# New cost figures for the planner of a hybrid encoder kernel: profiled durations in place of the old ones

## Chip, cores and metric

The kernel runs on one core of one Trainium2 chip. The metric is the device time of one execution in microseconds (us), lower is better. The engines are PE (matmul), DVE, ACT, POOL and SP, which issues the transfers.

## What is computed

Two sequences of 1024 tokens, 1024 wide, go through two layers with shared weights and a final RMSNorm. One layer, cut from the reference:

```python
hdn = rmsnorm(x, norm_g)
z = einsum('bsd,dp->bsp', hdn, w_in)      # 12 column blocks of 256
y_a = pool_mixer(a_v) * silu(a_g)         # multi-scale window means
y_b = dilated_attention(rope(b_q), rope(b_k), b_v) * silu(b_g)
y_c = s5_mixer(c_u) * silu(c_g)           # state-space scan, both directions, then a GLU
y_d = neighbourhood_attention(d_q, d_k, d_v, rpb) * silu(d_g)
return x + einsum('bsm,md->bsd', concatenate([y_a, y_b, y_c, y_d]), w_out)
```

Everything is 32-bit. The large products are made in three terms of a reduced type (fp32r): high times high, high times low, low times high.

## The kernel before

The work is four passes, numbered 0 to 3: layer 0 for both sequences, then layer 1 for both. In a pass the stages are recorded in this order (`STEPS`, L1659): neighbourhood attention ("na"), dilated attention ("dil"), the state-space scan ("ssm"), its GLU ("sout"), pooling, the next sequence's input, and the output projection in two halves. Passes 0 and 1 also hold a set-up of state-space tables for a layer (`ssm_setup`, L1181).

Nothing is issued while it is recorded. A `Recorder` notes every instruction with the tiles it reads and writes; `order()` (L304) then plays the program against five engines and a transfer queue and writes down in which order each engine gets its instructions; `emit` (L443) issues that order, every instruction from L461. Each engine executes its list strictly in that order, so a list is fixed before the chip sees it.

In that play an instruction holds its engine for `cost(op)` (L206), and a reader on another engine is ready `LAT` (L169) after that:

```python
op.end = now + op.cost            # L393
lat = LAT.get((e, o.eng), 130)    # L421
```

When an engine falls free it takes, of the instructions that are ready and whose tiles have room, the one of lowest priority number: its place in the recording, plus a large number (`LATE`, L475) for the long projections, which are so used as filler between the steps of the attention and scan chains. Filler is limited by tiles, by weights (three buffers of high parts, three of low) and by three PSUM banks; once issued it is gone for the stages behind it. `LAT` has, for instance, 142 ns from ACT to DVE, 127 from DVE to DVE and 640 from DVE to PE, and 1100 + 900 ns around a transfer.

The scan stage (`ssm_in`, L1444) works on four "quads" of groups in each pass. For a quad PE makes 16 products of `UM` and `B` into two PSUM banks (`pp`; the two banks of pool "s"). DVE reads them in four multiplications with `R` into `X` and a scratch tile, makes two sums and two scans over 512 columns, POOL multiplies `X` with `R` twice, DVE twice in place, and four DVE instructions write `H`. PE then multiplies `H` with `Cm` and `M` (the second half of `UM`) with `UM`. The set-up makes four groups: six DVE instructions of 512 columns for `W`, eight transposes of it on PE, six DVE instructions of 576 columns for `R`, eight small products of `R` on PE.

Names in profile and lists are those of the buffer's first user: `vz` is one of three PSUM banks for projections, `kt` one of two banks for scores and `pp`, `ss` and `rb` the two banks for transposes and for the scan's output, `no` the one for attention outputs; `xh`, `xl`, `whi`, `wlo` are halves of input and weight, and `wto`, `zq`, `zs`, `kt`, `th` also name the scratch tiles of 512 columns.

Of the kernel before, what the change touches and what calls it, by code (L numbers as in the profile page):

```python
# [176 lines left out]
class Recorder:  # L177
# [26 lines left out]
        self.threads.append(self.thread)  # L204

    def cost(self, op):  # L206
        out = op.writes[0]
        n = 1
        for _, c in out.dims[1:]:
            n *= c  # L210
        spaces = [v.tile.space for v in op.reads] + [out.tile.space]
        ps = "PSUM" in spaces
        if op.eng == "PE":
            if op.method == "transpose":
                return 107 * n / 128
            f32r = op.reads[0].dtype == F32R
            return n / 2.4 + 1 if f32r and n >= 256 else max(n, 128) / 0.6 + 1
        if op.eng == "DVE":
            m = op.method
            if m == "reciprocal":  # L220
                return 68 + 6.5 * n / 0.96
            if not ps and m in ("tensor_copy", "tensor_scalar", "tensor_scalar_mul", "memset"):
                return 66 + n * 0.525
            return 68 + n * 1.042 + (8 if m == "tensor_tensor_reduce" else 0) + (61 if isinstance(op.kw.get("scalar"), View) else 0)
        if op.eng == "ACT":
            return (52 if ps else 93) + n * 0.833 + (93 if "accum_out" in op.kw else 0) + (94 if len(op.reads) > 1 else 0)
        if op.eng == "POOL":
            if op.method == "memset":
                return 40 + n * 0.5
            spread = any(s == 0 and c > 1 for v in op.reads for s, c in v.dims[1:])  # L230
            return 148 + n * (1.67 if spread else 2.1)
        return 640

    def record(self, eng, method, args, kw):
# [243 lines left out]
SSMP, SB, GLU, POOLR, SPLIT, H0Z = (0, 1), "t", 0, 1, 'gpsimd', 1  # L478
# [1342 lines left out]
```

## Time and profile before

| | us |
|---|---|
| median of 3 runs (lowest, highest) | 2167.78 (2164.34, 2167.82) |
| the profiled execution | 2156.2 |
| its span, first to last instruction | 2154.4 |
| PE busy in the span | 1984.5 |
| DVE busy | 1572.2 |
| ACT busy | 1095.0 |
| POOL busy | 573.6 |

The busy time of PE is the union of matmuls whose recorded lengths overlap, so PE can be "busy" while it is fed at less than full rate. The table by stage further down sets each engine's busy time beside the length of the stage: the difference is idle time. A bracket in a timeline is idle time of that engine just before the row.

### The profile page before, as it was taken

The page shows a single profiled execution, that of the slowest core. Times are in us where ns is not written, and L with a number is a line of the kernel's source. Part 1 is how long each engine was busy: PE and PEld are TensorE (multiplying, and loading weights), DVE is VectorE, ACT ScalarE, POOL GpSimd, SP SyncE. Part 2 cuts the span into 40 slices and gives each one's busy share as a digit, 9 for nine tenths or more (in the row PEclk, how much of TensorE's full clock was granted, in tenths as well). Part 3 has the DMA queues.
Part 4 walks back from the last instruction along what each step waited for, and adds up shares of the span by engine and source line. Part 5 has one row for each costly group of instructions (what it writes and reads, how often), then busy time and mean ns, then how long its engine had stood idle before and what let it go on. Part 6 is the DMA issues. An engine that isn't in the chain of part 4 may idle for free.

```text
span 2154.4 us, 33356 instructions
## 1 busy us (share of the span) xinstructions
PE 1984.5 (92%) x10980; PEld 1656.8 (77%) x10980; DVE 1572.2 (73%) x3400; ACT 1095.0 (51%) x2486; POOL 573.6 (27%) x464
## 2 busy tenths in 40 slices
PE   7989999889999999889998999888899999998997
PEld 7757778667888888767787788767678878786777
DVE  7998688987246578788688667888734666888835
ACT  4438595134156688225125678823433766861315
POOL 3218231336200202124017142234543001202103
PEclk8999999999999999999999999999999999999999
DMA  4456535638855444646886543454588645346375
GB/s 160 147 167 188 169 95 169 191 106 269 270 168 160 134 145 118 202 134 217 265 250 187 175 151 105 129 180 155 197 283 278 214 144 173 106 139 201 115 243 178
DMA packets 321853, 381.12 MB, mean 177 GB/s; under 512 B 50832, under 2 KB 196752, under 8 KB 321680
## 3 DMA queue, kind: packets, MB, share of 16 engines
q1 hardware_dynamic: 321680, 378.99, 56.4%
q8 instruction: 87, 1.43, 0.3%
q14 instruction: 86, 0.70, 0.1%
HBM read 268.88 MB, written 112.10 MB: 177 GB/s over the span
## 4 chain that ended last, share of the span: by engine, by line
PE 44%; DVE 22%; DMA 14%; ACT 8%; issue 7%; POOL 3%; SPq 3%; DVEq 0%; POOLq 0%; ACTq 0%
PE vz L461 30%; DMA nv<-vd 4%; PE kt L461 4%; PE no L461 4%; DVE X L461 3%; DMA p<-x 3%; PE ss L461 3%; SPq L461 3%; PE rb L461 2%; DVE p L461 2%; DVE zq L461 1%; DVE gate L461 1%; DVE arena L461 1%; DVE H L461 1%; ACT p L461 1%
## 5 line engine op out<-in xcount | busy, mean ns | idle before, releaser
L461 PE MATMUL vz<-xh,whi 128*128 128x512 f32 x1324 | 531.7, 402 | 3.7 <-DVE zq L461 1.8
L461 PE MATMUL vz<-xl,whi 128*128 128x512 f32 x1324 | 531.5, 401 | 1.5 <-DVE xl L461 1.5
L461 PE MATMUL vz<-xh,wlo 128*128 128x512 f32 x1324 | 530.8, 401 | 0.8 <-POOL wlo L461 0.8
L461 POOL TENSOR_TENSOR wlo<-raw,whi 128x512 fp32r<-128x512 f32 x128 | 179.8, 1406 | 590.7 <-ACT whi L461 437.8
L461 ACT ACTIVATE whi<-raw 128x512 fp32r<-128x512 f32 x248 | 155.6, 627 | 340.5 <-DMA raw<-in_w_in 120.8
L461 PEld LDWEIGHTS vz<-xh,whi 128*128 128x128 f32 x1324 | 251.7, 190 | 49.9 <-issue 2.9
L461 PEld LDWEIGHTS vz<-xh,wlo 128*128 128x128 f32 x1324 | 251.8, 190 | 44.6 <-issue 2.1
L461 PEld LDWEIGHTS vz<-xl,whi 128*128 128x128 f32 x1324 | 252.2, 191 | 43.7 <-DVE xl L461 2.0
L461 PE MATMUL vz<-whi,xh 128*128 128x256 f32 x464 | 135.2, 292 | 15.1 <-ACT xh L461 8.6
L461 ACT ACTIVATE p<-p,st 128x256 f32<-128x256 f32 x256 | 128.3, 503 | 30.6 <-DVE st L461 29.3
L461 DVE TENSOR_TENSOR p<-vz,p 128x512 f32<-128x512 f32 x86 | 58.4, 687 | 112.8 <-DMA p<-x 96.8
L461 PE MATMUL vz<-whi,xl 128*128 128x256 f32 x464 | 134.2, 289 | 0.1
L461 PE MATMUL vz<-wlo,xh 128*128 128x256 f32 x464 | 133.8, 289 | 0.1
L461 PE MATMUL vz<-yh,whi 128*128 128x512 f32 x300 | 121.5, 405 | 9.6 <-DVE p L461 5.2
L461 PE MATMUL vz<-yl,whi 128*128 128x512 f32 x300 | 120.0, 400 | 0.0
L461 PE MATMUL vz<-yh,wlo 128*128 128x512 f32 x300 | 119.5, 400 | 0.0
L461 PEld LDWEIGHTS vz<-whi,xh 128*128 128x128 f32 x464 | 91.3, 197 | 16.9 <-ACT xh L461 8.6
L461 ACT ACTIVATE p<-p,nmx 128x384 f32<-128x384 f32 x128 | 78.2, 612 | 43.1 <-DVE nmx L461 42.1
L461 DVE TENSOR_TENSOR D<-ss,D 128x128 fp32r<-128x128 f32 (+2 forms) x195 | 85.5, 461 | 9.8 <-ACT D L461 8.2
L461 PEld LDWEIGHTS vz<-whi,xl 128*128 128x128 f32 x464 | 91.3, 197 | 1.0 <-issue 0.4
L461 PEld LDWEIGHTS vz<-wlo,xh 128*128 128x128 f32 x464 | 91.2, 197 | 0.8 <-issue 0.4
L461 PE MATMUL no<-D,bv 128*128 128x256 f32 x512 | 88.7, 293 | 3.1 <-DVE D L461 1.5
(489 smaller groups left out, 4616.1 us busy)
## 6 DMA issues: line engine op xcount, KB each, us to landing
raw<-in_w_in SPq DMA_DIRECT2D x192, 256.0 KB
low<-wlo SPq DMA_DIRECT2D x128, 256.0 KB
wlo<-low SPq DMA_DIRECT2D x120, 256.0 KB
x<-p SPq DMA_DIRECT2D x112, 256.0 KB
p<-x SPq DMA_DIRECT2D x88, 256.0 KB
nbias<-in_na_bias SPq DMA_DIRECT2D x48, 384.0 KB
nv<-vd SPq DMA_DIRECT2D x256, 64.0 KB
raw<-in_w_out SPq DMA_DIRECT2D x128, 128.0 KB
```

What stands on the lines that cost most here:

```text
L461: getattr(engines[op.eng], op.method)(*[real(a) for a in op.args], **{k: real(v) for k, v in op.kw.items()})
```

## The change

`cost` gets other figures, and nothing else is touched: not `LAT`, not the priorities, not the instructions. DVE gets 145 ns and 1.055 ns a column (68 and 1.042 before), 150 ns more where two operands of 256 columns or more lie in SBUF, 350 + 2.1 a column for a scan (priced like any other instruction before). ACT gets 180 or 205 ns of fixed cost (52 or 93 before). A 512-column matmul gets 226 ns (214 before), POOL 190 + 2.4 a column (148 + 2.1).

```diff
-        out = op.writes[0]
+
+        out, m = op.writes[0], op.method
...
         if op.eng == "PE":
-            if op.method == "transpose":
-                return 107 * n / 128
+            if m == "transpose":
+                return 108 * n / 128
             f32r = op.reads[0].dtype == F32R
-            return n / 2.4 + 1 if f32r and n >= 256 else max(n, 128) / 0.6 + 1
+            half = 0.7 if out.dims[0][1] == 64 else 1
+            return n / 2.4 + 13 if f32r and n >= 256 else half * (max(n, 128) / 0.6 + 9)
         if op.eng == "DVE":
-            m = op.method
+
+            wide = sum(v.tile.space == "SB" and v.dims[1:] != [[1, 1]] for v in op.reads) > 1
+            port = 150 if wide and n >= 256 else 0
             if m == "reciprocal":
-                return 68 + 6.5 * n / 0.96
+                return 145 + 6.1 * n
+            if m == "tensor_tensor_scan":
+                return 350 + 2.1 * n
             if not ps and m in ("tensor_copy", "tensor_scalar", "tensor_scalar_mul", "memset"):
-                return 66 + n * 0.525
-            return 68 + n * 1.042 + (8 if m == "tensor_tensor_reduce" else 0) + (61 if isinstance(op.kw.get("scalar"), View) else 0)
+                return 145 + n * 0.53
+            return 145 + n * 1.055 + port + (85 if m == "tensor_tensor_reduce" else 0) + (60 if isinstance(op.kw.get("scalar"), View) else 0)
         if op.eng == "ACT":
-            return (52 if ps else 93) + n * 0.833 + (93 if "accum_out" in op.kw else 0) + (94 if len(op.reads) > 1 else 0)
+            return (180 if ps else 205) + n * 0.833 + (187 if "accum_out" in op.kw else 0) + (88 if len(op.reads) > 1 else 0)
         if op.eng == "POOL":
-            if op.method == "memset":
-                return 40 + n * 0.5
+            if m == "memset":
+                return 90 + n * 0.84
             spread = any(s == 0 and c > 1 for v in op.reads for s, c in v.dims[1:])
-            return 148 + n * (1.67 if spread else 2.1)
+            return 190 + n * (1.8 if spread else 2.4)
```

The lists of all five engines change from their first rows on. Three places show how.

PE in the scan stage of pass 1, before: from the fourth quad's products to the row that reads the third quad's `H`.

```order
L461 MATMUL kt_1467<-UM_8725,B_8731 64x128 x8
L461 MATMUL vz_623<-UM_8725,B_8731 64x128 x8
L461 MATMUL vz_545<-xl_11_612,whi_644 128x512
L461 MATMUL vz_545<-xh_3_588,wlo_526 128x512
L461 MATMUL vz_545<-xh_4_663,whi_520 128x512
L461 MATMUL vz_545<-xl_12_679,whi_520 128x512
L461 MATMUL vz_545<-xh_4_663,wlo_792 128x512
L461 MATMUL vz_545<-xh_5_673,whi_520 128x512
L461 MATMUL rb_931<-H_8715,Cm_8710 128x128
```

Six projection matmuls stand here between the products and the first `H` row, and 65 between the third quad's first products and the fourth quad's `H`.

The same engine and stage after: the last row with the second quad's `H`, the fourth quad's products, the third quad's `H`.

```order
L467 MATMUL ss_693<-H_8685,Cm_8666 128x128 x2
L467 MATMUL vz_607<-UM_8807,B_8816 64x128 x8
L467 MATMUL kt_2298<-UM_8807,B_8816 64x128 x8
L467 MATMUL ss_693<-UM_8807 128x128
L467 MATMUL rb_940<-H_8805,Cm_8802 128x128 x2
```

The projection matmuls have gone from here to earlier places: the fourth quad's products are followed at once by the third quad's `H`, and 15 projection matmuls are left between the third quad's first products and the fourth quad's `H`.

DVE in that stage, before: from the fourth quad's second scan (the lists print a scan as SCALAR_TENSOR_TENSOR) to its `H`.

```order
L461 SCALAR_TENSOR_TENSOR X_8814<-zq_1100,X_8814 128x512
L461 TENSOR_TENSOR pu_8625<-vz_545,ss_4860 128x512
L461 SCALAR_TENSOR_TENSOR cs_8844<-cs_8844,cy_8811 128x1024
L461 TENSOR_TENSOR X_8814<-X_8814,R_1766_8737 128x512 x2
L461 TENSOR_TENSOR H_8807<-X_8814,zs_2230 64x4x127
L461 TENSOR_TENSOR H_8807<-X_8814,wto_1303 64x4x127
```

One instruction of pooling (`pu`) and one of the GLU stage (`cs`) stand here inside the chain.

DVE after: the fourth quad from its first sum, past both scans, to its `H`.

```order
L467 TENSOR_TENSOR X_8847<-X_8847,zs_2087 128x512
L467 SCALAR_TENSOR_TENSOR cs_8867<-cs_8867,cy_8849 128x1024
L467 SCALAR_TENSOR_TENSOR X_8847<-zq_1024,X_8847 128x512
L467 SCALAR_TENSOR_TENSOR cy_8849<-cs_8867,cy_8849 128x1024
L467 TENSOR_TENSOR wto_2167<-vz_607,R_1766_8824 128x512
L467 TENSOR_TENSOR X_8847<-X_8847,wto_2167 128x512
L467 SCALAR_TENSOR_TENSOR X_8847<-zq_1024,X_8847 128x512
L467 TENSOR_TENSOR X_8847<-X_8847,R_1766_8824 128x512
L467 SCALAR_TENSOR_TENSOR gate_7997<-zq_1024,zq_1367 128x512
L467 TENSOR_TENSOR X_8847<-X_8847,R_1766_8824 128x512
L467 TENSOR_TENSOR H_8875<-X_8847,zs_2087 64x4x127
L467 TENSOR_TENSOR H_8875<-X_8847,wto_2167 64x4x127
```

The `cy` instruction of the GLU stage, which stood behind the fourth quad's `H`, and a `gate` instruction now stand inside the chain; the third and fourth quads' steps are also interleaved more closely.

PE at the end of the first set-up, before: from a group's transposes of `W` to its products of `R`.

```order
L461 MATMUL rb_931<-c_ident_524,W_1778 128x128 x4
L461 MATMUL vz_543<-xh_6_722,wlo_792 128x512
L461 MATMUL vz_543<-xh_7_738,whi_520 128x512
L461 MATMUL vz_543<-xl_15_759,whi_520 128x512
L461 MATMUL vz_543<-xh_7_738,wlo_792 128x512
L461 MATMUL kt_1467<-R_1748,arena_630 32x128
L461 MATMUL kt_1467<-R_1810,arena_630 32x128
```

Projection matmuls stand here between a group's transposes and its products.

PE there after: the end of one group and the start of the next, its transposes and its first products.

```order
L467 MATMUL kt_2298<-R_2058,arena_614 32x128
L467 MATMUL kt_2298<-R_2404,arena_614 32x128
L467 MATMUL rb_940<-c_ident_524,W_2441 128x128 x8
L467 MATMUL kt_2298<-R_2422,arena_614 32x128
L467 MATMUL kt_2298<-R_2447,arena_614 32x128
```

The projections have moved ahead of this: the last three groups follow one another with none between.

## Rows read from the trace of the kernel before

**Rows 1.** Page, head and part 1: span, then busy time by engine.

```profile
span 2154.4 us, 33356 instructions
PE 1984.5 (92%) x10980; PEld 1656.8 (77%) x10980; DVE 1572.2 (73%) x3400; ACT 1095.0 (51%) x2486; POOL 573.6 (27%) x464
```

**Rows 2.** Page, part 4: the chain that ended last, by engine.

```profile
PE 44%; DVE 22%; DMA 14%; ACT 8%; issue 7%; POOL 3%; SPq 3%; DVEq 0%; POOLq 0%; ACTq 0%
```

**Rows 3.** Windows: start:end, length, busy PE, PEld, DVE, ACT, POOL, clock, DMA, GB/s.

```profile
45.00:160.00 115.00, 101.55 (x529) 80.32 (x528) 104.80 (x325) 48.73 (x108) 22.02 (x17) 0.94 0.53 155
160.00:365.00 205.00, 189.30 (x1166) 159.42 (x1165) 162.97 (x400) 155.44 (x406) 82.86 (x66) 1.00 0.49 148
365.00:440.00 75.00, 60.74 (x349) 50.22 (x349) 70.78 (x85) 11.39 (x21) 28.25 (x27) 0.94 0.59 188
...
610.00:880.00 270.00, 260.08 (x1515) 221.59 (x1514) 186.51 (x473) 193.33 (x491) 26.70 (x23) 0.99 0.47 138
880.00:950.00 70.00, 57.30 (x344) 48.19 (x343) 60.60 (x84) 11.53 (x19) 18.86 (x18) 0.93 0.60 196
...
1150.00:1405.00 255.00, 238.32 (x1388) 203.22 (x1389) 189.56 (x456) 186.40 (x480) 93.67 (x75) 0.98 0.47 146
1405.00:1490.00 85.00, 71.68 (x420) 57.99 (x417) 78.39 (x100) 13.99 (x24) 32.75 (x29) 0.96 0.55 169
...
1700.00:1925.00 225.00, 216.52 (x1285) 185.88 (x1283) 161.71 (x415) 171.49 (x442) 26.54 (x21) 0.99 0.47 140
1925.00:2000.00 75.00, 63.18 (x393) 52.19 (x392) 64.62 (x90) 11.84 (x21) 19.05 (x20) 0.93 0.61 191
```

**Rows 4.** Groups on PE, all forms apart: busy us, mean ns, idle before.

```profile
L461 PE MATMUL kt<-K,Qn 128*128 128x256 f32 x68 | 20.5, 315 | 8.2 <-ACT K L461 7.3 <-DVE st L461 0.5 <-ACT Qn L461 0.4
L461 PE MATMUL vz<-K,Qn 128*128 128x256 f32 x60 | 17.7, 310 | 3.4 <-ACT K L461 3.0 <-DVE st L461 0.3
```

**Rows 5.** Timeline of PE in pass 1: start, length, what, idle before.

```profile
895.19 1.09 PE L461 MATMUL vz<-UM,B 128*64 128x128 f32 x16
896.11 1.04 PE L461 MATMUL kt<-UM,B 128*64 128x128 f32 x16
...
913.00 0.39 PE L461 MATMUL vz<-xh,wlo 128*128 128x512 f32 x1
913.22 0.39 PE L461 MATMUL vz<-xh,whi 128*128 128x512 f32 x1
918.79 0.77 PE L461 MATMUL ss<-H,Cm 128*128 128x128 f32 x2 [5.18 <-issue]
...
922.26 0.61 PE L461 MATMUL ss<-H,Cm 128*128 128x128 f32 x4
922.70 0.39 PE L461 MATMUL ss<-UM 128*128 128x128 f32 x2
```

**Rows 6.** Timeline of DVE, same stage: start, length, what.

```profile
903.20 1.21 DVE L461 TENSOR_TENSOR bacc<-bacc,bacc 128x1024 f32<-128x1024 f32 x1
904.33 0.68 DVE L461 TENSOR_TENSOR X<-X,wto 128x512 f32<-128x512 f32 x1
...
933.36 0.68 DVE L461 TENSOR_TENSOR zs<-vz,R 128x512 f32<-128x512 f32 x1
933.96 0.68 DVE L461 TENSOR_TENSOR X<-vz,R 128x512 f32<-128x512 f32 x1
...
935.75 1.21 DVE L461 TENSOR_TENSOR_SCAN X<-zq,X 128x512 f32<-128x512 f32 x1
936.88 0.66 DVE L461 TENSOR_TENSOR X<-X,wto 128x512 f32<-128x512 f32 x1
```

**Rows 7.** All uses of tile X on DVE: duration min/median/max in ns.

```profile
L461 DVE TENSOR_TENSOR X<-X,R x32: 615/1512/1783, 374.1 to 1994.7; 128x512 f32<-128x512 f32 x32
```

**Rows 8.** Groups on DVE from 45 to 160 us: busy us, mean ns.

```profile
L461 DVE TENSOR_TENSOR W<-W,R 128x512 f32<-128x512 f32 x8 | 5.5, 682 | 0.1
L461 DVE TENSOR_TENSOR R<-R,W 128x576 f32<-128x576 f32 x8 | 6.5, 806 | 0.0
```

## The prediction

> **What bounds the kernel now.** I read the page's head and its chain first, then the busy time of each engine stage by stage, then single rows where a stage was idle.
>
> PE is busy 1984.5 of 2154.4 us and DVE 1572.2 [rows 1]; the chain that ended last lies 44% on PE, 22% on DVE and 14% on transfers [rows 2]. So PE sets the time overall, and what an order of the same instructions can win or lose is the time in which PE waits, 170 us. The table by stage says where that is [rows 3]. In the four stretches of scan, GLU and pooling (365 to 440, 880 to 950, 1405 to 1490 and 1925 to 2000 us) PE is idle 14.3, 12.7, 13.3 and 11.8 us, together 52.1; there DVE is busy 94, 87, 92 and 86% of the time: DVE is the bound, and PE keeps busy only as far as filler is left. In the four stretches of the attentions (160 to 365, 610 to 880, 1150 to 1405 and 1700 to 1925) PE is idle 15.7, 9.9, 16.7 and 8.5 us, together 50.8 of 955, with DVE at 69 to 79%. In the stretch of the first set-up (45 to 160) it is idle 13.5 us, DVE 91% busy. The other 54 us lie at the two ends and around the output projections.
>
> **What the new figures mean.** The profile shows a DVE instruction over 512 columns as 0.68 us long, but the next one starts 0.60 us after it: 933.36 and 933.96 [rows 6]. The old table has 68 + 512 x 1.042 = 602 ns for it, the spacing; the new one 685 ns with one operand in PSUM, 835 with two in SBUF, the recorded length and more. For a scan the old table has 602 ns, and the spacing is 1.13 us (935.75 to 936.88); the new one has 1425. For a 512-column matmul the spacing is 0.22 to 0.23 us (913.00 and 913.22) [rows 5]; here the new 226 ns is nearer than the old 214. The planner will thus rightly leave more room behind matmuls and scans, and wrongly believe DVE some quarter slower than it is. Filler goes wherever PE waits for a chain, so a plan with slower DVE spends more filler per step in the attentions, which come first, and has less for the scan, which comes last. The order shows that this is what happens.
>
> The Trainium skill speaks against this use of recorded lengths: Perfetto Trace Analysis, section Optimizing Scalar/DVE Operations, says that the recorded latency carries about twice the engine's overhead, because the write-acknowledging half overlaps the next instruction. The two DVE rows named above agree (0.68 long, 0.60 apart).
>
> **The sum, part by part.** Numbers of instructions are counted in the two orders, durations come from the rows.
>
> *Scan stage.* I take the piece between the third quad's first products on PE and the fourth quad's first `H` row, since DVE's work in it can begin only when those products end, and the `H` row can run only when that work has ended. Before, PE has 65 to 88 projection matmuls in this piece (15 to 20 us at 0.227) and DVE 35 to 40 instructions. After, PE has 15 in passes 1 to 3 and none in pass 0, and DVE has 41. What DVE needs: 33 instructions of 508 or 512 columns x 0.60 = 19.8; 3 of about 1024 columns x 1.13 (903.20 to 904.33) = 3.4; 5 scans x 1.13 = 5.7; together 28.9 us [rows 6]. What PE has: 15 x 0.227 = 3.4; 24 products of `UM` and `B` x 0.115 (895.19 to 896.11 for eight) = 2.8; 24 products with `H` or `M` x 0.22 (922.26 to 922.70 for two) = 5.3; 11.5 us, or 8.1 in pass 0 [rows 5]. PE must wait at least 17.4 us in each of three passes and 20.8 in pass 0: 73 us. On top come slower instructions. `X<-X,R`, two per quad, has a shortest length of 615 ns and a median of 1512 [rows 7]: it runs beside POOL's multiplications of the same tiles. Six of them in the piece x 0.83 us above the usual 0.68 = 5.0 a pass, 20 in all. So 93 us of waiting. The first two quads, which now have 18 to 27 us of PE work behind their products in place of 11 to 14, I take as covered. Against today's 52.1 us: **+41**. Lower end: no slowing, 73 - 52 = +21. Upper end: all six at the longest, 1783 ns, which is 6.6 a pass, and the first two quads keep a quarter of today's 52: 73 + 26 + 13 - 52 = +60.
>
> *Attention stages.* What left the scan stage covers waits here. The clearest one is the first scores of dilated attention, which wait 7.3 + 3.0 us for `K` from ACT [rows 4]: a quarter of them had under 12.8 us of PE work between the last projection of `K` and themselves, now only a tenth has under 24.5. I take all 10.3 us as saved. Of the remaining 40.5 us of idle time here I take a third, 13.5, since the work between a score and its transposes grows (median 7.4 to 8.4 us) but that between the transposes and the products that use them shrinks (5.0 to 4.2): **-24**. Ends: 10 us saved, or 40 (four fifths of all idle time there).
>
> *First set-up.* After, its last three groups stand on PE with no projection between. A group costs DVE 6 x 0.60 for `W` and 6 x 0.73 for `R` (682 and 806 ns long, 0.08 less as spacing [rows 8]), 8.0 us; its 16 small PE instructions, priced like those of the scan stage at 0.11, take 1.8. That leaves 6.2 a group, 19 for three, plus 2.5 for copies between: 21.5 against the 13.5 of today, **+8**. Ends: +3, if only 16.5 remain, and +18, if most of today's waits stay beside it.
>
> *The rest*: 0. SP issues the same transfers in another order. The PE work between a score that releases a load of `nv` and its use has a lower quartile of 16.5 us in place of 22, that ahead of a new projection weight 13.8 in place of 15.1; ACT's and POOL's figures move too, but neither engine is busy over 76% in any of the stretches read [rows 3]. I cover these by the 54 us of idle time outside the three kinds of stretch, which filler may shorten as well, and put 6 us either way.
>
> Sum: 41 - 24 + 8 = +25 us on the profiled 2156.2, hence 2181. That execution is 11.6 us under the median of the runs shown, 2167.78, which I take as the base: **2193 us**. By the lengths of the rows in place of their spacings the scan piece would be 41 x 0.08 = 3.3 us a pass longer, 2206.
>
> **Rivals.**
>
> *Faster: more room pays more than it costs.* The waits of the attentions fall by four fifths (-40), the set-up stays even, and the scan stage only reaches its lower end (+21): -19, 2149 us. For it: 51 us of idle time lie in stages that get filler, and scans and matmuls are now priced nearer the truth. Against it: the 73 us of the scan stage follow from counts and spacings alone. It decides once the saving in the attentions exceeds what the scan stage adds.
>
> *Same: filler only moves waits.* A scan stage at its lower end (+21), the attentions at the forecast (-24), the set-up at +3: 2168.
>
> *Slower still: the scan stage starves what follows.* GLU and pooling read what these chains make and have no filler of their own; if the first two quads keep half their waits (+26) beyond the forecast: 2219. For it: the granted clock in these stretches is 0.93 to 0.96 against 0.98 to 1.00 in the attentions [rows 3], so idle time costs some speed after it. It counts within slower.
>
> **How the numbers follow.** The forecast and the case beyond it have 0.70 (0.55 and 0.15), the faster rival 0.19, the same 0.11. About 0.2%, 4.3 us, is what a measurement of this kernel can tell from no change. The lower ends together give 21 - 40 + 3 = -16, with the 6 us of the rest -22; the upper ones 60 - 10 + 18 + 6 = +74. A tenth of the chance on each side is cut off: -12 to +60, 2156 to 2228.
>
> **What would show it.** The scan stretches should show 80 to 110 us of idle PE in place of 52.1, nearly all ahead of the third and fourth quads' `H` rows, in two waits a pass of 6 to 12 us, with DVE busy throughout. The attention stretches should show under 35 us of idle time and almost none on the scores that wait for `K`; around the last set-up groups three waits of about 6 us. I am wrong if the waits ahead of the last `H` rows sum to under 60 us, or if the attentions lose more idle time than the scan stages gain.

## The result, and the profile after

The changed kernel takes 2246.94 us (median of 4 runs, 2242.42 to 2252.87) beside 2166.06 us for the kernel before on the same chip (4 runs, 2162.55 to 2167.82): a ratio of 1.0382, 95% interval 1.0351 to 1.0412. It is slower by 81 us, where 25 were forecast and the range ended at 2228.

The head of the page, after; it answers to [rows 1]:

```profile
span 2251.1 us, 33433 instructions
PE 1997.8 (89%) x10980; PEld 1679.9 (75%) x10980; DVE 1580.2 (70%) x3400; ACT 1110.7 (49%) x2486; POOL 590.6 (26%) x464
```

The instructions are the same, and PE is busy 13.3 us longer and idle 83.4 us longer (253.3 in place of 169.9); the two make up the 96.7 us by which this span is longer than that of [rows 1]. The medians differ by 81 only: of the two profiled executions the one before lies 9.9 us under its median and the one after 5.9 over. The chain that ended last can be followed back only to 586 us here, so that its shares sum to 74% and can't be set beside those of [rows 2].

For the ledger the spans are cut where the work changes, not at equal times: at the first product and at the last output product of each scan. First the kernel before (columns as in [rows 3]; pass 0 up to the scan, the attentions of passes 1 to 3, and by itself the first set-up):

```profile
0.00:358.00 358.00, 315.98 (x1829) 266.20 (x1830) 294.56 (x802) 218.98 (x534) 122.90 (x101) 0.96 0.51 155
...
579.00:872.00 293.00, 283.08 (x1686) 244.77 (x1684) 186.91 (x475) 200.91 (x506) 28.18 (x23) 0.99 0.49 146
...
1094.00:1404.00 310.00, 291.40 (x1747) 247.97 (x1745) 239.64 (x584) 202.13 (x509) 106.56 (x84) 0.98 0.53 161
...
1629.00:1925.00 296.00, 286.03 (x1708) 247.59 (x1706) 201.11 (x502) 203.69 (x512) 34.18 (x28) 0.99 0.55 170
...
78.00:146.00 68.00, 61.61 (x332) 46.50 (x329) 62.75 (x131) 29.45 (x64) 10.79 (x8) 0.96 0.48 129
...
sum 323.00, PE 270.91 PEld 222.72 DVE 287.92 ACT 54.19 POOL 99.73; mean PE 67.73 PEld 55.68 DVE 71.98 ACT 13.55 POOL 24.93
```

The last row is the sum of the four scan stretches (358 to 444, 872 to 948, 1404 to 1490 and 1925 to 2000 us): PE is idle 52.1 us in them, as in the stretches of [rows 3].

The same view of the changed kernel, with its four scan stretches:

```profile
0.00:380.00 380.00, 330.77 (x1894) 282.76 (x1896) 302.16 (x802) 223.28 (x531) 131.04 (x104) 0.92 0.50 153
380.00:474.00 94.00, 57.63 (x354) 48.28 (x355) 71.21 (x101) 14.76 (x31) 26.82 (x24) 0.80 0.38 122
...
608.00:912.00 304.00, 295.04 (x1734) 256.87 (x1733) 188.88 (x470) 200.62 (x495) 30.62 (x24) 0.99 0.49 151
912.00:1006.00 94.00, 62.51 (x364) 51.31 (x364) 69.24 (x100) 15.48 (x30) 20.70 (x20) 0.79 0.40 124
...
1145.00:1471.00 326.00, 307.93 (x1817) 263.31 (x1817) 257.68 (x601) 203.58 (x500) 116.73 (x88) 0.98 0.54 164
1471.00:1563.00 92.00, 60.38 (x363) 49.72 (x360) 73.31 (x102) 15.76 (x32) 28.05 (x24) 0.80 0.39 124
...
1702.00:2007.00 305.00, 296.36 (x1758) 257.93 (x1757) 203.78 (x498) 202.06 (x498) 33.90 (x27) 1.00 0.54 172
2007.00:2099.00 92.00, 60.30 (x361) 49.44 (x362) 68.56 (x100) 15.21 (x31) 19.75 (x20) 0.81 0.40 125
...
139.00:217.00 78.00, 53.97 (x344) 42.96 (x342) 65.94 (x129) 36.20 (x75) 19.37 (x15) 0.81 0.44 117
```

Idle PE is length less busy PE, in us:

| stage | before | after | difference |
|---|---|---|---|
| four scans | 52.1 | 131.2 | +79.1 |
| first set-up | 6.4 | 24.0 | +17.6 |
| the rest of pass 0 up to its scan | 35.6 | 25.2 | -10.4 |
| attentions of passes 1 to 3 | 38.5 | 35.7 | -2.8 |
| all else | 37.3 | 37.2 | -0.1 |

So nearly all of it is the scan, and the saving in the attentions, which should have paid for a good part, is almost absent. In the scan stretches DVE is busy 74 to 80% of the time, less than before [rows 3], and PE's granted clock is 0.79 to 0.81 in place of 0.93 to 0.96.

The idle time is not spread evenly over a scan. Sums of the four stretches, first up to the third quad's first products (423.96, 955.61, 1512.51 and 2048.71 us), then from there on:

```profile
sum 170.79, PE 146.72 PEld 114.91 DVE 125.89 ACT 37.95 POOL 39.09; mean PE 36.68 PEld 28.73 DVE 31.47 ACT 9.49 POOL 9.77
...
sum 201.21, PE 94.11 PEld 83.84 DVE 156.41 ACT 23.27 POOL 56.23; mean PE 23.53 PEld 20.96 DVE 39.10 ACT 5.82 POOL 14.06
```

PE is idle 24.1 us in the first parts and 107.1 in the second, where it was 18.2 and 33.9 before, cut in the same way.

PE's timeline in the scan of pass 1, after: start, length, what, and in brackets the idle time before it.

```profile
955.61 1.09 PE L467 MATMUL kt<-UM,B 128*64 128x128 f32 x16
...
959.95 0.39 PE L467 MATMUL vz<-xh,wlo 128*128 128x512 f32 x1
...
967.67 1.35 PE L467 MATMUL ss<-H,Cm 128*128 128x128 f32 x4 [5.89 <-issue]
...
976.35 1.97 PE L467 MATMUL kt<-UM,B 128*64 128x128 f32 x16 [2.52 <-DVE zq L467]
980.46 0.77 PE L467 MATMUL ss<-UM 128*128 128x128 f32 x2 [2.14 <-DMA UM<-Md]
984.30 1.35 PE L467 MATMUL rb<-H,Cm 128*128 128x128 f32 x4 [3.07 <-issue]
...
1001.00 1.35 PE L467 MATMUL ss<-H,Cm 128*128 128x128 f32 x4 [11.51 <-issue]
...
1005.85 0.78 PE L467 MATMUL vz<-xh,whi 128*128 128x512 f32 x1
```

The last filler before the gap is the projection at 959.95, the next one starts at 1005.85. Between them PE has the products of the last quads and waits. The rows at 967.67, 984.30 and 1001.00 begin the output of the second, third and fourth quad. The chain of waits over the same stretch says for what (start, length, what):

```profile
967.67 5.15 PE ss L467 x22
...
972.89 0.61 ACT zq L467
...
973.51 2.00 DMA yd<-zq
...
975.60 0.70 DVE zq L467
...
977.15 2.20 POOL zq L467
...
979.37 1.74 DVE X L467
...
984.30 5.21 PE rb L467 x22
...
989.59 0.61 ACT wto L467
...
990.21 2.00 DMA yd<-wto
...
992.31 0.70 DVE wto L467
...
1001.00 5.19 PE ss L467 x22
```

The quads run one behind the other. PE's output products of a quad end, ACT copies them into a scratch tile (`ys`, here under the name `zq`, then `wto`), a transfer reads that tile (2.00 us), and only then may DVE write the same tile as `H0` of the next quad, whose `H` PE waits for. From 967.67 to 984.30 and on to 1001.00 the rounds take 16.6 and 16.7 us, 5.2 of them PE's own products.

The gates of GLU and pooling and the input of pooling have 288 projection matmuls in a pass. Where the two orders put them on PE, over the four passes:

| | ahead of the scan's first product | in the scan | behind it |
|---|---|---|---|
| before | 0 | 150 to 179 | 109 to 138 |
| after | 61 to 71 | 97 to 107 | 120 |

By this count the scan lost 43 to 75 projections a pass and 61 to 71 went ahead of it, so the filler did move early. But about as many as before, 120, or 27 us of PE a pass at 0.227, still lay behind the scan while PE stood idle in it, and these were not drawn in. Something in the plan held them back. A gate's projection leaves its PSUM bank into a scratch tile (`zg`), one of the six from which the scan's chain takes `H0`, `r8b` and `ys`; then ACT needs a second scratch tile (`th`) to go on. Three gate halves of the GLU stage show it in pass 1, after. DVE empties the bank into the scratch tile in the first three rows, and ACT reads that tile in the last three (`ss` is the name of the tile of scales here):

```profile
895.60 0.69 DVE L467 SCALAR_TENSOR_TENSOR zq<-vz,ss 128x512 f32<-128x512 f32 x1 [0.19 <-PE vz L467]
...
905.68 0.69 DVE L467 SCALAR_TENSOR_TENSOR th<-vz,ss 128x512 f32<-128x512 f32 x1 [0.34 <-PE vz L467]
...
931.81 0.69 DVE L467 SCALAR_TENSOR_TENSOR zr<-vz,ss 128x512 f32<-128x512 f32 x1
...
995.15 0.63 ACT L467 ACTIVATE zq<-zq 128x512 f32<-128x512 f32 x1 [4.96 <-DVE X L467]
998.45 0.63 ACT L467 ACTIVATE zq<-th 128x512 f32<-128x512 f32 x1 [2.67 <-DVE gate L467]
1001.58 0.63 ACT L467 ACTIVATE wto<-zr 128x512 f32<-128x512 f32 x1 [2.51 <-DVE H L467]
```

They hold three of the six tiles for 99.6, 92.8 and 69.8 us and can't go on, while the scan uses the other three or the plan keeps them for it. In `order()`'s own play two of the three banks stay full behind them and the third is left empty, so that no other projection begins; in its play of the kernel before, no gate there waits over 7 us for its second tile.

### The profile page after: what moved, and what is told of

It reads as the page before. It is cut to its first block, busy times and chain, and to the rows that moved or that the text cites. A ratio compares the mean times of both kernels' runs of the same rounds, so it can differ in the third digit from the quotient of the medians.

```text
span 2251.1 us, 33433 instructions
## 1 busy us (share of the span) xinstructions
PE 1997.8 (89%) x10980; PEld 1679.9 (75%) x10980; DVE 1580.2 (70%) x3400; ACT 1110.7 (49%) x2486; POOL 590.6 (26%) x464
## 3 DMA queue, kind: packets, MB, share of 16 engines
q1 hardware_dynamic: 321680, 378.99, 53.4%
## 4 chain that ended last, share of the span: by engine, by line
PE 44%; DMA 13%; DVE 9%; issue 3%; SPq 2%; ACT 2%; POOL 1%; DVEq 0%; ACTq 0%; POOLq 0%
PE vz L467 30%; PE kt L467 4%; DMA nv<-vd 4%; PE no L467 4%; PE ss L467 3%; DMA p<-x 3%; PE rb L467 3%; SPq L467 2%; DVE X L467 1%; DVE gate L467 1%; DVE p L467 1%; DMA bf<-f 1%; DVE xl L467 1%; DVE bacc L467 1%; DMA p<-in_x 1%
## 5 line engine op out<-in xcount | busy, mean ns | idle before, releaser
L467 PE MATMUL vz<-whi,xh 128*128 128x256 f32 x432 | 125.4, 294 | 10.9 <-ACT xh L467 8.7
L467 PE MATMUL vz<-whi,xl 128*128 128x256 f32 x432 | 126.0, 292 | 0.7 <-DVE xl L467 0.6
L467 PE MATMUL vz<-wlo,xh 128*128 128x256 f32 x432 | 125.5, 292 | 0.0
L467 DVE TENSOR_TENSOR D<-rb,D 128x256 fp32r<-128x256 f32 (+2 forms) x220 | 94.2, 448 | 15.9 <-ACT D L467 12.5
L467 ACT ACTIVATE D<-rb 128x256 fp32r<-128x256 f32 (+2 forms) x220 | 83.5, 406 | 28.0 <-PE rb L467 24.8
L467 PE MATMUL ss<-H,Cm 128*128 128x128 f32 x128 | 34.9, 425 | 69.9 <-issue 57.8
L467 PEld LDWEIGHTS vz<-whi,xh 128*128 128x128 f32 x432 | 85.9, 200 | 12.5 <-ACT xh L467 8.7
L467 PE MATMUL rb<-c_ident,p 128*128 128x128 f32 x490 | 87.7, 277 | 3.3 <-ACT p L467 3.3
```

The lines of the kernel that those rows point to most:

```text
L467: getattr(engines[op.eng], op.method)(*[real(a) for a in op.args], **{k: real(v) for k, v in op.kw.items()})
```

## Experiments

Theory A: the filler that is left is held up by scratch tiles, as just told. Theory B: the prediction's, filler spent because DVE is believed slow. The kernels that mix the tables hold both bodies of `cost`, as `old_cost` and `new_cost`, and choose by engine or by stage; their diffs show that one line. "Idle" is PE idle in the four scan stretches, cut as in the ledger (52.1 before, 131.2 after).

| run | us | ratio to before (95% interval) | idle |
|---|---|---|---|
| new_gate_in_place | 2198.28 | 1.0154 (1.0107 to 1.0200) | 27.5 |
| old_gate_in_place | 2173.52 | 1.0034 (1.0015 to 1.0054) | 54.0 |
| new_act_only | 2292.64 | 1.0587 (1.0552 to 1.0621) | 129.7 |
| new_dve_only | 2182.07 | 1.0065 (1.0045 to 1.0084) | 58.0 |
| act_gate_in_place | 2168.86 | 0.9999 (0.9977 to 1.0022) | 53.4 |
| new_attn_only | 2229.14 | 1.0275 (1.0226 to 1.0324) | 106.6 |
| new_not_attn | 2139.10 | 0.9872 (0.9825 to 0.9918) | 15.9 |
| new_setup_scan | 2129.60 | 0.9825 (0.9787 to 0.9864) | 13.6 |
| new_ys_in_X | 2190.83 | 1.0114 (1.0084 to 1.0144) | 89.8 |
| act_dil_only | 2266.40 | 1.0469 (1.0440 to 1.0499) | 127.3 |
| new_scan_only | 2130.59 | 0.9835 (0.9804 to 0.9865) | 17.2 |
| setup_scan_less_scratch | 2129.73 | 0.9847 (0.9810 to 0.9884) | 14.8 |
| all_but_act_dil | 2183.12 | 1.0093 (1.0064 to 1.0122) | 32.0 |
| new_less_scratch | 2214.49 | 1.0236 (1.0211 to 1.0261) | 21.8 |
| spacing_table | 2193.84 | 1.0131 (1.0101 to 1.0161) | 43.9 |

**Is the filler spent or held up?** All new figures, and a gate that needs no scratch tile to empty its bank:

```diff
-            z, th = self.z("zg"), self.z("th")
+            z, th = g[:, sl], self.z("th")
```

> All new figures, and one tile less: a gate's projection is scaled out of its PSUM bank into the gate's own tile instead of into a scratch tile. Theory A (held up): in the changed kernel the projections of the gates and of pooling were not spent early; they stood still because a bank can only be emptied into one of the six scratch tiles, which the scan's chain held, so that all three banks stayed full. The bank now needs no scratch tile; the order has 82 to 117 projection matmuls (0 before) behind the third quad's products and 86 to 91 behind the fourth's. It expects PE idle in the four scan stretches of 60 us or less in place of 131, and 2165 to 2205 us in place of 2247. Theory B (the prediction's: filler spent early in the attentions, 73 us of wait owed to DVE's work alone): what was spent does not come back, the waits move, 2235 to 2255.

The control is the same edit on the old figures.

> Control: the old figures with the same one tile less. Both theories: the scratch tiles were not short in the old plan, so 2166 within 8 us. If this is faster by 15 us or more, the edit helps by itself and the other run says less about the figures.

50 of the 81 us come back (31 are left over before on the same chip); the control is 0.3% slower. Windows of the run with the new figures, the scan of pass 1 and what stands behind it up to the next pass:

```profile
899.00:988.00 89.00, 81.59 (x494) 67.47 (x490) 78.01 (x117) 23.91 (x46) 18.66 (x22) 0.96 0.57 177
988.00:1135.00 147.00, 123.63 (x533) 95.50 (x534) 108.97 (x272) 45.35 (x69) 36.98 (x21) 0.92 0.64 205
```

PE runs 494 matmuls in this scan in place of 364, idle 7.4 us in place of 31.5. In this order 57 to 65 projections a pass still stand ahead of the scan, but 223 to 231 within it and none behind. So theory A holds for the scan, with one correction: projections did go ahead, and it is not these that the scan lacked, but those that were held up. The price is in the second row: 23.4 us idle behind the scan, where 7 were lost before and after, because with no projection left nothing stands beside the GLU; the waits of PE over the whole run show it (us in total, times, longest):

```profile
PE vz L467 <- DMA gw<-in_glu_w: 26.4, 4, 8.1
```

**Which engine's figures?**

```diff
+        return self.new_cost(op) if op.eng in ('ACT',) else self.old_cost(op)
```

(with `'DVE'` in the second run, and with the gate in place besides in the third)

> New figures for ACT alone (180 or 205 ns fixed in place of 52 or 93), old ones for all others. Theory A (held up by the gate's chain DVE - ACT - DVE, which holds a scratch tile from its first to its last instruction): ACT's figures alone lengthen that hold; the order has only 7 to 19 projection matmuls behind the third and the fourth quad's products. It expects 2200 to 2245 us, with scan stretches of 80 us or more of idle PE. Theory B (prediction: DVE believed too slow is what moves filler): within 15 us of 2166.

> New figures for DVE alone, old ones for all others. Theory B (prediction): this is the cause, so most of the +81 us: 2215 to 2250. Theory A: in this order the third and fourth quads of passes 1 to 3 have 91 to 107 projection matmuls behind their products, only pass 0 has 0 and 18; it expects one starved scan stage of four, about 20 us, and up to 15 us at the set-up: 2180 to 2205.

> New figures for ACT alone, and the gate's projection scaled into the gate's own tile. Theory A (held up): with ACT alone the waits lay in pooling (its weights' high halves come late from ACT, since the three buffers stay full while the projections before them stand in full banks). Without the scratch tile the order has 46 to 67 projection matmuls behind the third and the fourth quad's products: from 2293 back to 2165 to 2200 us, and the 30 us that pooling's projections wait in each pass fall under 10. Theory C (ACT's figures hurt by another way, such as where its weight splits stand in its own list): 2240 us or more.

DVE's figures, on which the prediction argued, cost 15 us. In the run with them alone one scan stretch of four starves, as expected: 45 of the 58 us of idle time are in pass 0. ACT's figures alone cost 126, more than all together and more than theory A had allowed: PE is idle 276 us in all (2008.3 busy of 2284.2), 106 more than before, of which 78 lie in the scans. The gate edit brings that run back from 2292.64 to 2168.86, with idle time in the scans at 53.4, as before: for ACT's figures by themselves the scratch tile is all of it. PE's and POOL's figures were not tried alone.

**Which stage?**

```diff
+        return self.new_cost(op) if op.thread.name.startswith(("na_", "dil_")) else self.old_cost(op)
```

(the complement has `not` in front; the others name `("ssm_","setup")`, `"ssm_"`, and ACT in `"dil_"`)

> New figures for the instructions of neighbourhood and dilated attention only, old ones elsewhere. Theory B (the prediction's: attentions that are believed slow spend the filler): all of it comes from here, 2230 us or more, with the attentions' waits down by 20 us. Theory A: the order has no projection behind the third and 19 behind the fourth quad's products in passes 0, 1 and 3, but 68 and 79 in pass 2; the hold-up needs a gate that begins inside dilated attention and then finds its scratch tiles taken, which these figures bring about: 2195 to 2240.

> The complement: new figures everywhere but in the two attentions. Theory A and B: filler is kept for the scan (the order has 64 to 108 projection matmuls behind the third and the fourth quad's products in place of 24 to 55): faster than 2166, 2130 to 2160. Theory D (the scan's, set-up's and pooling's own new figures do harm): 2175 or more.

> New figures only in the set-up and in the scan stage: what the change would be if only the two stages in which DVE is the bound were repriced. The order has 65 to 109 projection matmuls behind the third and the fourth quad's products. Theory A: scan waits fall from 73 to under 45 us, set-up waits to under 10, nothing else moves: 2125 to 2155. Theory D: 2166 or more.

> New figures in the scan stage alone; the set-up keeps the old ones. The order has 64 to 107 projection matmuls behind the third and the fourth quad's products (before: 26 to 55). Scan waits 73 down to 25 to 45 us, set-up unchanged: 2130 to 2160. If the gain of the run with both (2129.6) came from the set-up: 2160 or more.

> New figures for one engine in one stage: ACT in dilated attention; old ones elsewhere. Theory A (the plan then sees PE idle in dilated attention, begins the next gates there, and they are the ones that find their scratch tiles taken): the order has 58 to 91 gate and pooling projections ahead of the scan's first products (none with the old figures) and 0 to 10 behind the third quad's: 2225 to 2290, as bad as all new figures together. If the scan's or pooling's own figures were needed for the loss: 2185 or less.

The stages fall on opposite sides. New figures in the attentions alone cost 61 us, and ACT's in dilated attention alone 99 us (the first of the two runs lies just where the expectations of A and B meet and decides little; the second shows that ACT's figures in one stage are enough for the loss). Everywhere but in the attentions they gain 29, in set-up and scan alone 38, in the scan alone 37. The orders say how: with ACT repriced in dilated attention 58 to 91 gate and pooling projections stand ahead of the scan and 100 behind it; with set-up and scan repriced none stands ahead, 219 to 233 within and 55 to 69 behind. The scan of pass 1 in the run with set-up and scan repriced (windows):

```profile
875.00:953.00 78.00, 77.54 (x475) 64.57 (x475) 70.87 (x103) 17.46 (x28) 18.58 (x22) 1.00 0.65 206
```

PE is idle for 0.5 us in it, DVE busy 91%. This version, the new table in the set-up and the scan only, beats both kernels, the one before by 1.8%; with the scan alone repriced the time is the same within the noise.

**Is that trigger needed?** All new figures except ACT's in dilated attention:

```diff
+        return self.new_cost(op) if not (op.eng == "ACT" and op.thread.name.startswith("dil_")) else self.old_cost(op)
```

> All new figures but one engine in one stage: ACT in dilated attention keeps the old ones. Theory A (that is the trigger, and needed): the order has 10 gate and pooling projections ahead of the scan's first products (61 to 71 in the changed kernel) and 25 to 60 behind the scan (120): the scan's waits fall from 156 to under 70 us; set-up stays where it is; 2165 to 2205. If the other figures hold the gates up as well: 2225 or more.

62 of the 81 us go with it (19 are left over before on the same chip), and idle time in the scans falls to 32.0.

**Why was the scan's wait larger than its work?** All new figures, with `ys` in a tile that is dead by then:

```diff
-            ys = self.z("ys")
+            ys = X[:, 0]
```

> All new figures; the copy of the scan's output (ys) goes into the first half of X, which is dead by then, and no longer into a scratch tile that the next quad's H0 must wait for until the transfer yd<-ys has read it. The filler is as in the changed kernel: no projection behind the third quad's products in pass 0, 15 in the others, none behind the fourth's; DVE's work is the same. Theory S (the scan's wait was undersized because each quad waits for the scratch tile of the one before, so that DVE's work starts late): 25 to 60 us less than the changed kernel, 2185 to 2222, with DVE busier in the scan stretches than the 66 to 71 us of 87 to 90 it has now. Theory W (the wait is DVE's own work plus half clock on PE after each wait): within 12 us of 2247.

57 us less, with the same fillers in the same stretches. Windows of its four scans, to be set beside those of the changed kernel:

```profile
382.00:463.00 81.00, 56.75 (x348) 47.58 (x347) 66.36 (x92) 14.94 (x31) 25.57 (x24) 0.81 0.46 141
900.00:980.00 80.00, 56.99 (x362) 46.36 (x362) 66.18 (x92) 15.73 (x31) 18.97 (x18) 0.89 0.48 143
1436.00:1515.00 79.00, 57.94 (x362) 47.68 (x361) 68.22 (x93) 16.44 (x34) 25.52 (x24) 0.85 0.47 144
1959.00:2039.00 80.00, 58.51 (x365) 47.96 (x364) 65.12 (x93) 15.89 (x31) 20.16 (x20) 0.86 0.47 146
```

12 to 14 us shorter each, idle 89.8 together in place of 131.2, DVE busy 81 to 86%. So 41 us of the idle time hung on that one tile, which ACT's copy and the transfer hold until the next quad may write it, and not on DVE's work. All of it lies from the third quad's first products on, where PE is idle 64.6 us in place of 107.1; ahead of them it is 25.2 in place of 24.1. The same edit on the kernel before was not tried.

**Do the parts add up?** Both edits on all new figures, and both on the fastest mixture:

> All new figures with both edits, gate in its own tile and ys in X: what the figures cost where scratch tiles are not short. The order has 0 to 4 of 288 projections left behind the scan, so nothing covers the GLU: its waits stay near the 69 us of the run with the gate alone. 2185 to 2205, about that run's 2198; under 2180 if the scratch tiles were all of it.

> New figures in set-up and scan, the gate in its own tile and ys in X: the best of the pieces together. If the scratch tiles still bound the scan with these figures: 2100 to 2125. If the figures alone had freed them already (55 to 69 of 288 projections are left behind the scan in either case): 2125 to 2140, the same as without the two edits.

They do not. Idle time in the scans is lowest of the runs with all new figures, 21.8, and the time is worse than with either edit alone. Sum of the windows of the four stretches behind the scans (462 to 592, 983 to 1130, 1542 to 1690 and 2064 to 2208 us):

```profile
sum 569.00, PE 461.83 PEld 350.99 DVE 360.63 ACT 190.60 POOL 168.77; mean PE 115.46 PEld 87.75 DVE 90.16 ACT 47.65 POOL 42.19
```

PE is idle 107 us there. Nearly all filler went into the scan or ahead of it (0 to 4 projections a pass are left behind it), and the stages behind starved instead. With the mixture the edits change nothing: with its figures the scratch tiles were not what bound the scan.

**Are lengths in place of spacings the fault?** DVE by the old table, but a scan at its spacing, ACT nearly by the old table, PE and POOL as in the change (the lines of DVE's other instructions, not shown here, go back to the old figures):

```diff
-                return 350 + 2.1 * n
+                return 58 + 2.1 * n
...
-            return (180 if ps else 205) + n * 0.833 + (187 if "accum_out" in op.kw else 0) + (88 if len(op.reads) > 1 else 0)
+            return (52 if ps else 108) + n * 0.833 + (93 if "accum_out" in op.kw else 0) + (88 if len(op.reads) > 1 else 0)
```

> A table by the spacing from one start to the next: DVE and ACT as in the old table, but a scan at 1.13 us and ACT reading SBUF at 108 ns plus 0.833 a column; PE and POOL as in the change. If the loss came from recorded lengths taken for spacings, as the prediction's premise has it: 2150 to 2172. If any shift of the figures loses the old table's luck: 2185 or more.

A miss for the first expectation: 30 us slower than before, though idle time in the scans is 43.9. The time lies in the range of the other one, that any shift of the figures loses what the old order had; that not every shift does is shown by the runs that gain. PE is busy 18 us longer and idle 18 us longer (2002.5 of 2190.7), the latter spread over the other stretches. A table that is nearer to the spacings is not better by that. Why this one loses was not followed further; PE's and POOL's new figures are in it.

## Why the prediction was wrong in size and in cause

By spans 25 us were forecast and 96.7 measured. Of the 71.7 between them 38 are in the scan's term, 11 in that of the attentions, 10 in the set-up's and 13 in PE's busy time, which had no term.

**Direction and place were right**: slower, and by the scan. Ahead of the third and the fourth quads' `H` PE waits 79.6 us over the four passes, above the 60 under which the prediction called itself wrong; 11.5 a pass lie ahead of the fourth, and the rest is in several pieces ahead of the third. In time the slower rival, 2219, was nearer than the forecast. Of what it rests on, the first two quads keep waits, but its GLU does not starve (idle time behind the scan of pass 1 is 7.5 us before and 6.9 after).

**The cause was not.** The step "filler goes wherever PE waits for a chain, so a plan with slower DVE spends more filler per step in the attentions" failed twice. The figures that matter are ACT's, 126 us alone against 15 for DVE's; and of them those in dilated attention, 99 us. I had read that "ACT's and POOL's figures move too", and put it into the rest at 0 because neither engine is busy; but a planner's figures act by the order they make, not by how busy the engine is. And what was spent early is not what the scan lacked. 61 to 71 projections a pass did move ahead, yet 120 stood behind the scan, and making the gate independent of the scratch tiles brought idle time in the scans to 27.5 with 57 to 65 still ahead. I had counted the projections in the one piece and never asked where the others stood. The Trainium skill's Perfetto Trace Analysis, section Identifying Performance Opportunities, says that the same gap repeating on the engine that should be saturated can mean that there is too little SBUF or PSUM for the next tile. The trace agrees: the gap ahead of the last quad's products (11.51 us in pass 1) comes in every scan, and an edit of one tile takes 104 of 131 us away. The scratch tiles and banks can be counted in the program beforehand.

**Scan stage, +41, measured +79.** The forecast's 93 us of idle time are for the piece from the third quad's first products on; measured there are 107. The other 24 us lie ahead of that piece, in the part of the first two quads that the sum took "as covered", at nothing. The 93 are near the 107 by luck, since two terms inside were wrong and offset each other. The hand-over of the scratch tile was left out: without it 64.6 us are left in the piece. And DVE was to be "busy throughout", with `X<-X,R` at its slow length in every quad of the piece; DVE is busy 156.4 of 201.2 us there, 78%, and the median of `X<-X,R` fell from the 1512 ns of [rows 7] to 691. Its row among the uses of tile X on DVE, after:

```profile
L467 DVE TENSOR_TENSOR X<-X,R x32: 671/691/1745, 411.4 to 2091.0; 128x512 f32<-128x512 f32 x32
```

**Attentions, -24, measured -13.** -10.4 are in pass 0 (with its start), -2.8 in the three others together. Filler there covered little. Waits of PE, after (us in total, times, longest):

```profile
PE rb L467 <- DVE W L467: 13.1, 5, 4.8
...
PE kt L467 <- DVE R L467: 8.7, 8, 2.3
PE kt L467 <- ACT K L467: 7.6, 4, 3.2
```

The last row was to be gone. With 0.9 us of the `vz` group, 8.5 of the 10.3 us of [rows 4] are still there. More PE work between a projection and its score, as the order shows it, took 1.8 us off these waits and not 10.3.

**Set-up, +8, measured +17.6.** The first two rows are the waits named, `W` and `R`, 21.8 us, in thirteen pieces and not in three. The mechanism was right: 24.0 us of idle time where 21.5 were forecast. The term was mis-sized by what was taken off, the 13.5 of a stretch of 115 us that held other work too; in the set-up itself only 6.4 had been idle.

**The rest, 0**, measured -0.1 in idle time. One term was not in the sum at all: PE is busy 13.3 us longer with the same instructions. Its cause stays open. The mean granted clock fell from 0.975 to 0.945, but PE's busy time does not follow it from run to run: with the spacing table it is 18 us longer at 0.972, and with `ys` in X it is that of the kernel before, 1984.2, at 0.959.

**Lengths against spacings.** The rows still show it, 0.68 long and 0.60 apart [rows 6], as the Trainium skill's Perfetto Trace Analysis, section Optimizing Scalar/DVE Operations, has it. But the use I made of it does not follow: DVE's longer figures cost little, and the table by spacings was slower as well.

## What to carry to other kernels

When a planner's figures move, don't stop at "filler is used earlier": count it ahead of, in and behind the stage that starves. If some is left behind an idle engine, look for what it must own to begin (a bank, the scratch tile that empties the bank, and the tile after that) and who holds it. A wait is bounded by the engine's work only if the buffers of successive rounds are free; follow one tile through copy, transfer and reuse before taking "engine busy throughout" for granted. And reprice one engine or one stage at a time: here ACT's new figures cost 99 us in one stage, and the whole new table gains 37 in another.

## What was not expected of the hardware

Behind its longer waits PE ran at half its clock for a while: the last three outputs of pass 1, behind waits of 3 to 11.5 us, took 5.15 to 5.21 us at a granted clock of 0.50 (1.2 GHz). One group of such an output starts 1.28 us after the one before (969.24 and 970.52), where it was 0.67 in the first quad's output, which stands in a stretch with filler (953.73 and 954.40). Directly after such an output it can be at 1.00 (2.4 GHz) again. The same products `UM,B` in pass 1, windows at 972.73, straight behind the second quad's output, and at 976.35, after 2.52 us of waiting:

```profile
972.73:973.80 1.07, 1.07 (x17) 0.85 (x16) 0.00 (x0) 0.60 (x1) 0.00 (x0) 1.00 0.00 0
...
976.35:978.30 1.95, 1.95 (x16) 1.57 (x16) 1.89 (x2) 0.00 (x0) 1.15 (x1) 0.50 0.70 190
```

In the other three passes the products behind the same wait of 2.5 us took 1.09 us, so that the wait just before them does not settle it. The 0.79 of the stretch is a mean of both levels. The four scans with filler ran at 0.98 to 1.00 in the run with set-up and scan repriced. So idle time in these scans cost more than the wait itself, some 2.4 us for an output at half clock, an estimate from four groups at 1.28 in place of 0.67 us.

The transfer of one `ys` tile took 2.00 us from ACT's end until DVE could go on, both times, which is 12% of a 16.7 us round.
